# Row standard deviation of an 8192 x 8192 matrix: a column split between VectorE and ScalarE, shrinking last pieces, contiguous loads, and results transposed on TensorE

## The chip, the core and the metric

The kernel runs on one core of a Trainium2 chip. Times are device microseconds (us), and a kernel's time is the median of several executions. The span is the time from the first to the last instruction in the profiled execution; here the median time is about 1.8 us more than the span. All runs that are compared are fast ones, with a granted clock of 1.0.

The program runs on several chips of the same kind, and the kernel before took 641.6, 642.6, 644.6 and 644.8 us in the four jobs of this study. So each variant is set beside the kernel before of its own job.

## The reference

```python
x = np.random.randn(8192, 8192).astype(np.float32)
def reference(x):
    return np.std(x, axis=1)
```

The input has 268.4 MB, the output 32 KB. Everything hangs on how fast x comes in (the page of the kernel before shows the DMA engines at 9 tenths or more in 38 of 40 slices), and on how little is left to do when its last byte has come.

## The kernel before

Partition p holds rows p*64 to p*64+63. One load brings row p*64+i of all 128 partitions, 4 MiB in 128 runs of 32 KiB that lie 2 MiB apart in memory. VectorE sums each row, ScalarE sums its squares in two halves. The last row comes as two halves.

```python
xrows = x.rearrange("(p i) m -> i p m", p=P, i=I)      # P = 128, I = 64, C = 8192, CS = 4096
out_pi = out.rearrange("(p i) -> p i", p=P)
rows = [(i, [0, C]) for i in range(I - 1)] + [(I - 1, [0, CS, C])]     # (shortened)
xpool = ctx.enter_context(tc.tile_pool(name="xtiles", bufs=5))
def do_row(i, cuts):
    # ...
    xt = xpool.tile([P, C], FP32, name="xt")
    for ci in range(len(cuts) - 1):
        c0, c1 = cuts[ci], cuts[ci + 1]
        nc.sync.dma_start(out=xt[:, c0:c1], in_=xrows[i][:, c0:c1])
        nc.vector.reduce_sum(out=asum[:, i - base, ci:ci + 1], in_=xt[:, c0:c1], axis=mybir.AxisListType.X)
        # ... for each piece of up to 4096 columns:
            nc.scalar.activation(out=dummy[:, 0:step], in_=xt[:, s0:s0 + step],
                                 func=Square, accum_out=asq[:, i - base, ci + si:ci + si + 1])
# ... variance of rows 0 to 61 on GpSimd while the last rows load; rows 62 and 63 on VectorE
nc.sync.dma_start(out=out_pi[:, 0:NB], in_=stdA)       # NB = 62: 128 runs of 248 bytes
# ...
nc.scalar.dma_start(out=out_pi[:, NB:I], in_=stdB)     # the last output: 128 writes of 8 bytes, 256 bytes apart
```

## Time and profile before

| | before |
|---|---|
| median time | 642.6 us (641.1 to 643.3, 4 runs) |
| span | 641.0 us |
| spacing of row tiles in the steady part | 9.72 us for 4 MiB |
| VectorE work for a tile | 8.69 us |
| ScalarE work for a tile | 2 x (3.59 + 0.19) us |
| last output, issue to end of span | 2.4 us |

From the page: the busy tenths of the 16 DMA engines and the rate in 40 equal slices of the span.

```profile
DMA  8999999999999999999999999999999999999992
GB/s 339 413 419 405 429 433 433 431 432 429 431 433 433 431 429 431 433 433 431 429 431 425 429 428 436 433 430 431 427 438 431 431 431 427 438 431 431 429 422 88
```

The load is busy from end to end: from the fifth slice to the last but one, the slices read 422 to 438 GB/s, and stretches of 80 to 160 us in the steady part 431 to 433. Only the first four slices (64 us, 339 to 419 GB/s) and the last one are slower. So I counted on no gain in the steady part. That was an estimate: no trace shows how far the rate could rise.

The two costly groups of the page: line, engine, operation, operands and count; busy time and mean of one in ns; idle time of the engine just before them and what ended it.

```profile
L58 DVE TENSOR_REDUCE sumA<-xt 128x1 f32<-128x8192 f32 x62 | 538.5, 8686 | 79.8 <-DMA xt<-in_x_dram 79.8
L67 ACT ACTIVATE dummy<-xt 128x4096 f32<-128x4096 f32 x128 | 459.2, 3587 | 156.1 <-DMA xt<-in_x_dram 154.0
```

Both engines wait for the load at each tile. They are off the critical path until the last tiles. (The page's chain still gives VectorE's reduces 16.3%, because a load is issued when a reduce has freed its buffer. But a load then takes 39.8 us from issue to landing, the time of four tiles, and the DMA engines' share is 0.98 to 1.01 in all stretches from 16 to 625 us: they have work queued throughout.)

VectorE's timeline at the start: start, duration, instruction, and in brackets the idle time before it.

```profile
14.14 8.69 DVE L58 TENSOR_REDUCE sumA<-xt 128x1 f32<-128x8192 f32 x1 [13.22 <-DMA xt<-in_x_dram]
25.27 8.69 DVE L58 TENSOR_REDUCE sumA<-xt 128x1 f32<-128x8192 f32 x1 [2.44 <-DMA xt<-in_x_dram]
34.98 8.69 DVE L58 TENSOR_REDUCE sumA<-xt 128x1 f32<-128x8192 f32 x1 [1.03 <-DMA xt<-in_x_dram]
45.23 8.69 DVE L58 TENSOR_REDUCE sumA<-xt 128x1 f32<-128x8192 f32 x1 [1.56 <-DMA xt<-in_x_dram]
55.51 8.69 DVE L58 TENSOR_REDUCE sumA<-xt 128x1 f32<-128x8192 f32 x1 [1.59 <-DMA xt<-in_x_dram]
66.17 8.69 DVE L58 TENSOR_REDUCE sumA<-xt 128x1 f32<-128x8192 f32 x1 [1.97 <-DMA xt<-in_x_dram]
75.89 8.69 DVE L58 TENSOR_REDUCE sumA<-xt 128x1 f32<-128x8192 f32 x1 [1.04 <-DMA xt<-in_x_dram]
```

A start here marks a tile's landing. The distances are 11.1, 9.7, 10.3, 10.3, 10.7 and 9.7 us: the load starts slowly and then runs evenly.

The end, from the timeline (the last three reduces merged, and the last output) and from the page's list of DMA issues (size, us from issue to landing):

```profile
620.38 17.34 DVE L58 TENSOR_REDUCE sumB<-xt 128x1 f32<-128x8192 f32 x3 [1.10 <-DMA xt<-in_x_dram]
638.58 0.37 ACTq L105 DMA_DIRECT2D out_dram<-stdB  x1
...
out_dram<-stdB ACTq DMA_DIRECT2D x1, 1.0 KB, 1.4
```

VectorE works 17.34 us without a pause from the landing of row 62, and the last output follows.

### The profile page before, as it was taken

The page shows a single profiled execution, that of the slowest core. Times are in us where ns is not written, and L with a number is a line of the kernel's source. Part 1 is how long each engine was busy: PE and PEld are TensorE (multiplying, and loading weights), DVE is VectorE, ACT ScalarE, POOL GpSimd, SP SyncE. Part 2 cuts the span into 40 slices and gives each one's busy share as a digit, 9 for nine tenths or more (in the row PEclk, how much of TensorE's full clock was granted, in tenths as well). Part 3 has the DMA queues.
Part 4 walks back from the last instruction along what each step waited for, and adds up shares of the span by engine and source line. Part 5 has one row for each costly group of instructions (what it writes and reads, how often), then busy time and mean ns, then how long its engine had stood idle before and what let it go on. Part 6 is the DMA issues. An engine that isn't in the chain of part 4 may idle for free.

```text
span 641.0 us, 576 instructions
## 1 busy us (share of the span) xinstructions
DVE 556.5 (87%) x72; ACT 477.9 (75%) x260; POOL 1.4 (0%) x8
## 2 busy tenths in 40 slices
DVE  1889889889889898898898898898898988988988
ACT  1767778778778778777787787787787787777886
POOL 0000000000000000000000000000000000000000
DMA  8999999999999999999999999999999999999992
GB/s 339 413 419 405 429 433 433 431 432 429 431 433 433 431 429 431 433 433 431 429 431 425 429 428 436 433 430 431 427 438 431 431 431 427 438 431 431 429 422 88
DMA packets 9653, 268.51 MB, mean 419 GB/s; under 512 B 1328, under 2 KB 1328, under 8 KB 1328
## 3 DMA queue, kind: packets, MB, share of 16 engines
q1 hardware_dynamic: 9504, 268.47, 97.9%
q14 instruction: 5, 0.04, 0.0%
q10 hardware_dynamic: 144, 0.00, 0.0%
HBM read 268.44 MB, written 0.03 MB: 419 GB/s over the span
## 4 chain that ended last, share of the span: by engine, by line
DMA 80%; DVE 19%; issue 1%; SPq 0%; ACT 0%; DVEq 0%
DMA xt<-in_x_dram 80%; DVE sumA L58 16%; DVE sumB L58 2%; SPq L57 0%; ACT stdB L103 0%; DVE vB L96 0%; DVE m L91 0%; DVE tsumB L89 0%; DVE tsqB L87 0%; DVEq L58 0%
## 5 line engine op out<-in xcount | busy, mean ns | idle before, releaser
L58 DVE TENSOR_REDUCE sumA<-xt 128x1 f32<-128x8192 f32 x62 | 538.5, 8686 | 79.8 <-DMA xt<-in_x_dram 79.8
L67 ACT ACTIVATE dummy<-xt 128x4096 f32<-128x4096 f32 x128 | 459.2, 3587 | 156.1 <-DMA xt<-in_x_dram 154.0
L67 ACT ACTIVATION_READ_ACCUMULATOR dummy<-xt 128x1 f32 x128 | 24.0, 187 | 0.0
L58 DVE TENSOR_REDUCE sumB<-xt 128x1 f32<-128x4096 f32 (+1 forms) x3 | 17.3, 5835 | 1.1 <-DMA xt<-in_x_dram 1.1
L103 ACT ACTIVATE stdB<-vB 128x2 f32<-128x2 f32 x1 | 0.2, 204 | 2.8 <-DVE vB L96 2.8
L67 ACT ACT_TABLE_LOAD x1 | 1.3, 1283 | 0.7 <-PEq L120 0.7
L80 POOL TENSOR_TENSOR tsqA<-sqA 128x62 f32<-128x62 f32 x1 | 0.3, 296 | 617.7 <-ACT dummy L67 617.7
L99 ACT ACT_TABLE_LOAD x1 | 1.3, 1283 | 0.0
L99 ACT ACTIVATE stdA<-vA 128x62 f32<-128x62 f32 x1 | 0.3, 257 | 1.0 <-POOL vA L84 1.0
L47 DVE MEMSET sumB<- 128x8 f32 x1 | 0.1, 65 | 0.8 <-PEq L120 0.8
L84 POOL TENSOR_TENSOR vA<-tsqA,t 128x62 f32<-128x62 f32 x1 | 0.3, 317 | 0.1
L82 POOL TENSOR_TENSOR t<-sumA 128x62 f32<-128x62 f32 x1 | 0.3, 295 | 0.9 <-DVE sumA L58 0.9
L83 POOL TENSOR_TENSOR t<-t,invn_t 128x62 f32<-128x62 f32 x1 | 0.3, 291 | 0.1
L96 DVE TENSOR_TENSOR vB<-tsqB,m 128x2 f32<-128x2 f32 x1 | 0.2, 161 | 0.0
L91 DVE SCALAR_TENSOR_TENSOR m<-tsumB 128x2 f32<-128x2 f32 x1 | 0.2, 160 | 0.0
L89 DVE TENSOR_REDUCE tsumB<-sumB 128x2 f32<-128x8 f32 x1 | 0.2, 161 | 0.0
L87 DVE TENSOR_REDUCE tsqB<-sqB 128x2 f32<-128x8 f32 x1 | 0.1, 149 | 0.0
L120 POOL MEMSET const-bfloat16-1.0<- 128x1 bf16 x1 | 0.1, 103 | 0.0
L120 POOL MEMSET const-uint8-127<- 128x1 uint8 x1 | 0.1, 103 | 0.0
L120 POOL MEMSET const-float32-0.0<- 128x1 f32 x1 | 0.1, 99 | 0.2 <-issue 0.2
L120 POOL MEMSET const-float32-1.0<- 128x1 f32 x1 | 0.1, 99 | 0.0
L48 DVE MEMSET sqB<- 128x8 f32 x1 | 0.1, 65 | 0.0
(1 smaller groups left out, 0.1 us busy)
## 6 DMA issues: line engine op xcount, KB each, us to landing
xt<-in_x_dram SPq DMA_DIRECT2D x63, 4096.0 KB, 39.8
xt<-in_x_dram SPq DMA_DIRECT2D x2, 2048.0 KB, 37.6
out_dram<-stdA SPq DMA_DIRECT2D x1, 31.0 KB, 9.8
out_dram<-stdB ACTq DMA_DIRECT2D x1, 1.0 KB, 1.4
```

The lines of the kernel that those rows point to most:

```text
L58: nc.vector.reduce_sum(out=asum[:, i - base, ci:ci + 1], in_=xt[:, c0:c1], axis=mybir.AxisListType.X,)
L67: nc.scalar.activation(out=dummy[:, 0:step], in_=xt[:, s0:s0 + step], func=mybir.ActivationFunctionType.Square, accum_out=asq[:, i - base, ...
L80: nc.gpsimd.tensor_add(tsqA, sqA[:, :, 0], sqA[:, :, 1])
L82: nc.gpsimd.tensor_mul(t0, sumA[:, :, 0], sumA[:, :, 0])
L83: nc.gpsimd.tensor_mul(t0, t0, invn_t.to_broadcast((P, NB)))
L84: nc.gpsimd.tensor_sub(vA, tsqA, t0)
L89: nc.vector.reduce_sum(out=tsumB, in_=sumB, axis=mybir.AxisListType.X)
L91: nc.vector.scalar_tensor_tensor(out=m2, in0=tsumB, scalar=inv_n, in1=tsumB, op0=mybir.AluOpType.mult, op1=mybir.AluOpType.mult,)
L96: nc.vector.tensor_sub(vB, tsqB, m2)
L99: nc.scalar.activation(out=stdA, in_=vA, func=mybir.ActivationFunctionType.Sqrt, scale=inv_n)
L103: nc.scalar.activation(out=stdB, in_=vB, func=mybir.ActivationFunctionType.Sqrt, scale=inv_n)
L120: nc = _bacc.Bacc("TRN2", target_bir_lowering=False, num_devices=1)
```

## The change

Three things change together. First, rows go to partitions as i*128+p, so one load reads 4 MiB in one piece, and results must be transposed (on TensorE) to be written as rows. Second, the columns of each row are split: VectorE takes 5120 as ten bn_stats of 512 (each leaves six numbers per partition) and one bn_aggr (which merges them into mean and variance), ScalarE 3072 (Square and Copy, each with an accumulator). Third, row 62 comes in halves and row 63 in pieces of 2048, 2048, 2048, 1024, 512, 256 and 256 columns, so that little work is left after the last landing. The intent is a faster start, a lighter VectorE and a short tail.

```diff
-    xrows = x.rearrange("(p i) m -> i p m", p=P, i=I)
-    out_pi = out.rearrange("(p i) -> p i", p=P)
+    xr = x.rearrange("(i p) m -> p i m", p=P, i=I)
+    out_ip = out.rearrange("(i p) -> i p", p=P)
+    ACT_ROW = 3072
+    pieces = [(i, 0, C, ACT_ROW) for i in range(I - 2)]
+    pieces += [(I - 2, 0, C // 2, ACT_ROW // 2), (I - 2, C // 2, C // 2, ACT_ROW // 2)]
+    for n, a in ((2048, 512), (2048, 512), (2048, 512), (1024, 0), (512, 0), (256, 0), (256, 0)):
+        pieces.append((LAST, c0, n, a))
+        c0 += n
-    xpool = ctx.enter_context(tc.tile_pool(name="xtiles", bufs=5))
+    bulk = ctx.enter_context(tc.tile_pool(name="bulk", bufs=4))
+    ends = ctx.enter_context(tc.tile_pool(name="ends", bufs=1))
 ... (per piece)
-            nc.vector.reduce_sum(...)
-                nc.scalar.activation(..., func=Square, accum_out=...)     # two of 4096
+        for d0 in range(a, n, F):                                        # F = 512
+            nc.vector.bn_stats(out=bn[:, k * SD:(k + 1) * SD], in_=xt[:, d0:d1])
+        if a:
+            nc.scalar.activation(out=dump[:, :a], in_=xt[:, :a], func=ACTF.Square, accum_out=q_act[:, r, j:j + 1])
+            nc.scalar.activation(out=dump[:, :a], in_=xt[:, :a], func=ACTF.Copy, accum_out=s_act[:, r, j:j + 1])
+        if c0 + n == C and r < LAST:
+            nc.vector.bn_aggr(out=agg[:, r, :], in_=bn)
+        if c0 + n == C and r == LAST - 1:
+            ... (11 small GpSimd operations give the variance of rows 0 to 62)
+            nc.scalar.activation(out=std, in_=t4, func=ACTF.Sqrt, scale=1.0 / N)
+            nc.tensor.transpose(std_ps, std, ident)
+            nc.scalar.copy(out=std_t, in_=std_ps)
+            nc.sync.dma_start(out=out_ip[0:B, :], in_=std_t)             # rows 0 to 62
 ... (ScalarE's part of row 63 joins VectorE's on GpSimd)
+    nc.vector.bn_aggr(out=agg[:, LAST, :], in_=last_bn)
+    nc.scalar.activation(out=stdl, in_=agg[:, LAST, 1:2], func=ACTF.Sqrt)
+    nc.scalar.dma_start(out=out_ip[LAST, :].rearrange("(p o) -> p o", o=1), in_=stdl)
```

Row 63's results are not transposed. They leave from 128 partitions, 4 bytes from each, to 128 addresses in 512 bytes.

More of the change, by code (lines that the diff above doesn't have):

```diff
@@ L9 @@
 FP32 = mybir.dt.float32
+ACTF = mybir.ActivationFunctionType
+ALU = mybir.AluOpType
 @with_exitstack
@@ L23 @@
     N = float(C)
-    inv_n = 1.0 / N
-    CS = C // 2
-    xrows = x.rearrange("(p i) m -> i p m", p=P, i=I)
-    out_pi = out.rearrange("(p i) -> p i", p=P)
-    NB = I - 2
-    rows = []
-    for i in range(I - 1):
-        rows.append((i, [0, C]))
-    rows.append((I - 1, [0, CS, C]))
-    xpool = ctx.enter_context(tc.tile_pool(name="xtiles", bufs=5))
+    F = nc.vector.BN_STATS_FMAX
+    SD = nc.vector.BN_STATS_DIM
+    LAST = I - 1
+    xr = x.rearrange("(i p) m -> p i m", p=P, i=I)
+    out_ip = out.rearrange("(i p) -> i p", p=P)
@@ L37 @@
+    ACT_ROW = 3072
+    pieces = [(i, 0, C, ACT_ROW) for i in range(I - 2)]
+    pieces += [(I - 2, 0, C // 2, ACT_ROW // 2), (I - 2, C // 2, C // 2, ACT_ROW // 2)]
+    c0 = 0
+    for n, a in ((2048, 512), (2048, 512), (2048, 512), (1024, 0), (512, 0), (256, 0), (256, 0)):
+        pieces.append((LAST, c0, n, a))
+        c0 += n
+    N_D = float(C - ACT_ROW)
+    bulk = ctx.enter_context(tc.tile_pool(name="bulk", bufs=4))
+    ends = ctx.enter_context(tc.tile_pool(name="ends", bufs=1))
     stats = ctx.enter_context(tc.tile_pool(name="stats", bufs=1))
+    bnp = ctx.enter_context(tc.tile_pool(name="bnp", bufs=3))
@@ L38 @@
     psum = ctx.enter_context(tc.tile_pool(name="psumdump", bufs=1, space=bass.MemoryType.PSUM))
-    dummy = psum.tile([P, CS], FP32)
-    NT = I - NB
-    sumA = stats.tile([P, NB, 4], FP32)
-    sqA = stats.tile([P, NB, 4], FP32)
-    sumB = stats.tile([P, NT, 4], FP32)
-    sqB = stats.tile([P, NT, 4], FP32)
-    nc.vector.memset(sumB, 0.0)
-    nc.vector.memset(sqB, 0.0)
-    invn_t = stats.tile([P, 1], FP32)
-    nc.vector.memset(invn_t, inv_n)
-    def do_row(i, cuts):
-        asum, asq, base = (sumA, sqA, 0) if i < NB else (sumB, sqB, NB)
-        xt = xpool.tile([P, C], FP32, name="xt")
-        for ci in range(len(cuts) - 1):
-            c0, c1 = cuts[ci], cuts[ci + 1]
-            nc.sync.dma_start(out=xt[:, c0:c1], in_=xrows[i][:, c0:c1])
-            nc.vector.reduce_sum(
-                out=asum[:, i - base, ci:ci + 1],
-                in_=xt[:, c0:c1],
-                axis=mybir.AxisListType.X,
-            )
-            nsub = (c1 - c0 + CS - 1) // CS
-            step = (c1 - c0) // nsub
-            for si in range(nsub):
-                s0 = c0 + si * step
-                nc.scalar.activation(
-                    out=dummy[:, 0:step],
-                    in_=xt[:, s0:s0 + step],
-                    func=mybir.ActivationFunctionType.Square,
-                    accum_out=asq[:, i - base, ci + si:ci + si + 1],
-                )
@@ L74 @@
-    vA = stats.tile([P, NB], FP32)
-    for (i, cuts) in rows:
-        do_row(i, cuts)
-        if i == NB - 1:
-            tsqA = stats.tile([P, NB], FP32)
-            nc.gpsimd.tensor_add(tsqA, sqA[:, :, 0], sqA[:, :, 1])
-            t0 = stats.tile([P, NB], FP32)
-            nc.gpsimd.tensor_mul(t0, sumA[:, :, 0], sumA[:, :, 0])
-            nc.gpsimd.tensor_mul(t0, t0, invn_t.to_broadcast((P, NB)))
-            nc.gpsimd.tensor_sub(vA, tsqA, t0)
-    tsqB = stats.tile([P, NT], FP32)
-    nc.vector.reduce_sum(out=tsqB, in_=sqB, axis=mybir.AxisListType.X)
@@ L88 @@
-    tsumB = stats.tile([P, NT], FP32)
-    nc.vector.reduce_sum(out=tsumB, in_=sumB, axis=mybir.AxisListType.X)
-    m2 = stats.tile([P, NT], FP32)
-    nc.vector.scalar_tensor_tensor(
-        out=m2, in0=tsumB, scalar=inv_n, in1=tsumB,
-        op0=mybir.AluOpType.mult, op1=mybir.AluOpType.mult,
-    )
-    vB = stats.tile([P, NT], FP32)
-    nc.vector.tensor_sub(vB, tsqB, m2)
-    stdA = stats.tile([P, NB], FP32)
-    nc.scalar.activation(out=stdA, in_=vA,
-                         func=mybir.ActivationFunctionType.Sqrt, scale=inv_n)
@@ L101 @@
-    nc.sync.dma_start(out=out_pi[:, 0:NB], in_=stdA)
-    stdB = stats.tile([P, NT], FP32)
-    nc.scalar.activation(out=stdB, in_=vB,
-                         func=mybir.ActivationFunctionType.Sqrt, scale=inv_n)
-    nc.scalar.dma_start(out=out_pi[:, NB:I], in_=stdB)
+    dump = psum.tile([P, ACT_ROW], FP32)
+    agg = stats.tile([P, I, 2], FP32)
+    s_act = stats.tile([P, I, 3], FP32)
+    q_act = stats.tile([P, I, 3], FP32)
+    nc.gpsimd.memset(s_act, 0.0)
+    nc.gpsimd.memset(q_act, 0.0)
@@ new lines @@
+    ident = stats.tile([P, P], FP32)
+    nc.gpsimd.memset(ident, 1.0)
+    nc.gpsimd.affine_select(out=ident, in_=ident, compare_op=ALU.is_equal, fill=0.0,
+                            base=0, pattern=[[-1, P]], channel_multiplier=1)
+    warm = stats.tile([P, 1], FP32)
+    nc.vector.memset(warm, 1.0)
+    nc.scalar.activation(out=warm, in_=warm, func=ACTF.Sqrt)
+    n_last = sum(-(-(n - a) // F) for r, _, n, a in pieces if r == LAST)
+    a_last = float(sum(a for r, _, n, a in pieces if r == LAST))
@@ new lines, with load, g @@
+    last_bn = stats.tile([P, 3 + n_last * SD], FP32)
+    def load(pi):
+        r, c0, n, _ = pieces[pi]
+        if n == C:
+            xt = bulk.tile([P, C], FP32, name="xt")
+        else:
+            xt = ends.tile([P, n], FP32, name=f"xe{pi}")
+        nc.sync.dma_start(out=xt, in_=xr[:, r, c0:c0 + n])
+        return xt
+    tiles = {}
+    bn, k, j = None, 0, 0
+    for pi, (r, c0, n, a) in enumerate(pieces):
+        if n == C:
+            tiles[pi] = load(pi)
+        elif pi not in tiles:
+            for ahead in range(pi, len(pieces)):
+                tiles[ahead] = load(ahead)
+        xt = tiles.pop(pi)
+        if c0 == 0:
+            k, j = 0, 0
+            if r < LAST:
+                bn = bnp.tile([P, (C - ACT_ROW) // F * SD], FP32, name="bn")
+            else:
+                bn = last_bn[:, 3:]
+        for d0 in range(a, n, F):
+            d1 = min(n, d0 + F)
+            nc.vector.bn_stats(out=bn[:, k * SD:(k + 1) * SD], in_=xt[:, d0:d1])
+            k += 1
+        if a:
+            nc.scalar.activation(out=dump[:, :a], in_=xt[:, :a], func=ACTF.Square,
+                                 accum_out=q_act[:, r, j:j + 1])
+            nc.scalar.activation(out=dump[:, :a], in_=xt[:, :a], func=ACTF.Copy,
+                                 accum_out=s_act[:, r, j:j + 1])
+            j += 1
+        if c0 + n == C and r < LAST:
+            nc.vector.bn_aggr(out=agg[:, r, :], in_=bn)
+        if c0 + n == C and r == LAST - 1:
+            B = LAST
+            def g(nm):
+                return stats.tile([P, B], FP32, name=nm)
+            dm, dv = agg[:, 0:B, 0], agg[:, 0:B, 1]
+            ss, qq, t1, t2, t3, t4 = (g(f"g{z}") for z in range(6))
+            nd = stats.tile([P, 1], FP32)
+            nc.gpsimd.memset(nd, N_D)
+            ndb = nd.to_broadcast((P, B))
+            ninv = stats.tile([P, 1], FP32)
+            nc.gpsimd.memset(ninv, 1.0 / N)
+            ninvb = ninv.to_broadcast((P, B))
+            nc.gpsimd.tensor_add(ss, s_act[:, 0:B, 0], s_act[:, 0:B, 1])
+            nc.gpsimd.tensor_add(qq, q_act[:, 0:B, 0], q_act[:, 0:B, 1])
+            nc.gpsimd.tensor_mul(t1, dm, dm)
+            nc.gpsimd.tensor_add(t1, t1, dv)
+            nc.gpsimd.tensor_mul(t1, t1, ndb)
+            nc.gpsimd.tensor_add(t1, t1, qq)
+            nc.gpsimd.tensor_mul(t2, dm, ndb)
+            nc.gpsimd.tensor_add(t2, t2, ss)
+            nc.gpsimd.tensor_mul(t3, t2, t2)
+            nc.gpsimd.tensor_mul(t3, t3, ninvb)
+            nc.gpsimd.tensor_sub(t4, t1, t3)
+            std = stats.tile([P, B], FP32)
+            nc.scalar.activation(out=std, in_=t4, func=ACTF.Sqrt, scale=1.0 / N)
+            std_ps = psum.tile([B, P], FP32)
+            nc.tensor.transpose(std_ps, std, ident)
+            std_t = stats.tile([B, P], FP32)
+            nc.scalar.copy(out=std_t, in_=std_ps)
+            nc.sync.dma_start(out=out_ip[0:B, :], in_=std_t)
+        if r == LAST and pi + 1 < len(pieces) and pieces[pi + 1][3] == 0 and a:
+            sl = stats.tile([P, 2], FP32)
+            an = stats.tile([P, 1], FP32)
+            nc.gpsimd.memset(an, 1.0 / a_last)
+            nc.gpsimd.memset(last_bn[:, 0:1], a_last)
+            nc.gpsimd.tensor_add(sl[:, 0:1], s_act[:, r, 0:1], s_act[:, r, 1:2])
+            nc.gpsimd.tensor_add(sl[:, 0:1], sl[:, 0:1], s_act[:, r, 2:3])
+            nc.gpsimd.tensor_add(sl[:, 1:2], q_act[:, r, 0:1], q_act[:, r, 1:2])
+            nc.gpsimd.tensor_add(sl[:, 1:2], sl[:, 1:2], q_act[:, r, 2:3])
+            nc.gpsimd.tensor_mul(last_bn[:, 1:2], sl[:, 0:1], an)
+            m2 = stats.tile([P, 1], FP32)
+            nc.gpsimd.tensor_mul(m2, last_bn[:, 1:2], sl[:, 0:1])
+            nc.gpsimd.tensor_sub(last_bn[:, 2:3], sl[:, 1:2], m2)
@@ L109 @@
+    nc.vector.bn_aggr(out=agg[:, LAST, :], in_=last_bn)
+    stdl = stats.tile([P, 1], FP32)
+    nc.scalar.activation(out=stdl, in_=agg[:, LAST, 1:2], func=ACTF.Sqrt)
+    nc.scalar.dma_start(out=out_ip[LAST, :].rearrange("(p o) -> p o", o=1), in_=stdl)
 _INS = ['x']
```

## The prediction

> **What bounds it now.** Loading x. The page's slices show the DMA engines at 9 tenths or more in 38 of 40; the table of stretches gives 432 GB/s from 160 to 320 us. In the timeline a row tile (4 MiB) arrives every 9.72 us. VectorE needs 8.69 us for it and ScalarE 2 x (3.59 + 0.19) = 7.6 us, so both wait for the DMA on each tile (idle before the groups: 79.8 and 156.1 us, ended by the DMA). Three pieces make up the 641.0 us span:
> - start: the first reduce begins at 14.1 us and the next come 11.1, 9.7, 10.3, 10.3, 10.7 us apart before the spacing settles at 9.72. The stretches show 340, 412, 420, 406, 428 GB/s up to 80 us. Against 9.72 that loses about 3.5 us, plus about 2 us before the first tile;
> - steady stream: 64 x 9.72 = 622 us;
> - tail: by the bytes in the stretches, data stop at about 628.4 us; I estimate landing at 630 (row 62's reduce started 1.6 us after its bytes by the same count). The other 11 us are VectorE's backlog (8.7 + 4.4 + 4.4 us, ending 637.7), tiny operations, Sqrt, and 2.4 us of output DMA.
>
> **What the change does.** Per row VectorE gets 5120 columns as ten bn_stats of 512. From the reduces (4409 ns for 4096, 8686 for 8192, so 1.044 ns a column plus about 0.13 us) I estimate 0.60 to 0.67 us each, 6.0 to 6.9 us with bn_aggr. ScalarE does 3072 columns twice: 2 x (2.74 + 0.19) = 5.9 us. Both were off the path already: no gain in the steady part. Four buffers still leave two transfers queued.
>
> Layout: a transfer now reads one contiguous 4 MiB instead of 128 rows 2 MiB apart. [...] this load runs at 432 GB/s at that pitch. [...] The layout may recover part of the 3.5 us start loss, whose cause the trace does not show; I count 1.5 us.
>
> Tail: the last row arrives in pieces down to 256 columns, so VectorE ends within about 1 us of landing. But ScalarE works in order: the Sqrt and PSUM copy for rows 0 to 62 stand before row 63's second and third pieces. Row 62 lands 9.7 us before the end; bn_stats 3.4, nine GpSimd operations at 0.37 = 3.4, Sqrt, transpose and copy about 1.5: ScalarE resumes 1.4 us before the last landing, needs 4 x 0.8 us, then GpSimd about 1.5 us, bn_aggr, Sqrt, output 2.5 us: about 6.7 us after landing instead of 11. Gain 4.3 us, less 0.5 us for small pieces.
>
> **Sum.** 642.8 - 4.3 + 0.5 - 1.5 = about 637.5 us; range 632.5 to 640.5. Faster by over 2% 0.05, within 2% 0.93, slower by over 2% 0.02.
>
> **What the profile would show.** Steady spacing still 9.7 us; VectorE about 6.5 us per tile, ScalarE 5.9; first tiles closer together if the layout matters; the chain of waits ending through ScalarE, GpSimd, bn_aggr, Sqrt and the output, 5 to 8 us after the last landing.
>
> **What would make it wrong.** bn_stats at half my rate would make VectorE the limit (over 11 us a tile). [...]

## The result, and the profile after

The changed kernel takes 643.6 us (643.3 to 643.9, 4 runs) against 642.6. The ratio is 1.0021, 95% interval 1.0006 to 1.0036. A ratio is the mean time of one kernel's fast runs over that of the other's of the same rounds, so it is not quite the ratio of the medians. The change gained nothing. The time is above the predicted range of 632.5 to 640.5.

The slices of the DMA engines and the rate:

```profile
DMA  9999999999999999999999999999999999999990
GB/s 372 445 425 423 435 443 429 423 431 439 435 425 427 433 441 431 425 427 437 441 425 427 431 438 433 429 425 433 439 433 427 423 439 439 427 427 431 430 383 11
```

The start is faster (372 and 445 for 339 and 413), and the rate in the steady part is the same (432 GB/s from 80 to 560 us, for 431 to 433). The groups:

```profile
L92 DVE BATCH_NORM_STATS2 bn<-xt 128x6 f32<-128x512 f32 x620 | 373.9, 678 | 213.4 <-DMA xt<-in_x_dram 213.4
L95 ACT ACTIVATE dump<-xt 128x3072 f32<-128x3072 f32 x62 | 169.6, 2735 | 257.7 <-DMA xt<-in_x_dram 257.7
```

VectorE's own work shrank to 6.03 us for ten bn_stats and 0.43 us for bn_aggr per tile, and it waits more (213.4 us before the bn_stats, for 79.8 before the reduces). That was off the path: between the steps described below, tiles still come 9.7 us apart. VectorE's timeline at the start and around one later tile:

```profile
13.07 6.03 DVE L92 BATCH_NORM_STATS2 bn<-xt 128x6 f32<-128x512 f32 x10 [12.13 <-DMA xt<-in_x_dram]
...
51.91 6.03 DVE L92 BATCH_NORM_STATS2 bn<-xt 128x6 f32<-128x512 f32 x10 [3.22 <-DMA xt<-in_x_dram]
...
62.31 6.03 DVE L92 BATCH_NORM_STATS2 bn<-xt 128x6 f32<-128x512 f32 x10 [3.91 <-DMA xt<-in_x_dram]
...
159.47 6.03 DVE L92 BATCH_NORM_STATS2 bn<-xt 128x6 f32<-128x512 f32 x10 [3.22 <-DMA xt<-in_x_dram]
...
170.15 6.03 DVE L92 BATCH_NORM_STATS2 bn<-xt 128x6 f32<-128x512 f32 x10 [4.19 <-DMA xt<-in_x_dram]
```

The fifth tile lands 3.6 us earlier than before (51.91 for 55.51). But where the wait is usually 3.22 us, it is once 3.91 and then, about every 114 us, 4.19: the steps come before the tiles that start at 62.3, 170.2, 287.7, 395.6 and 513.2 us. They cost 0.7 + 4 x 0.97 = 4.6 us. By row 61 the lead is nearly gone: its work starts at 610.32, against 610.60 before.

What comes at these moments? The page lists the trace's DMA queue 14 as "instruction", with packets, MB and share of time. First the changed kernel's lines of 51 to 56 us, then of 163 to 166 us:

```profile
q14 instruction: 1, 0.01, 0.4%
...
q14 instruction: 1, 0.01, 0.7%
```

Each of the two stretches holds one 8 KB instruction packet. The trace's packet records, in the page's clock, put such packets at 52.3, 163.8, 281.4, 389.3, 506.9 and 618.8 us. The first five last 0.32 to 0.33 us, and the next 32 KiB packet of x behind each takes 1.875 us instead of 1.21 (the sixth falls among the small packets of the end): together the 0.97 us of a step (0.32 + 0.66). Up to 507 us they are on average 113.6 us apart; VectorE issues 11 instructions per 9.72 us, so I estimate about 128 of them for a packet, or 64 bytes each (8192 / 128). The page counts ten such packets in all. The other four stand at 124.2, 375.2, 378.7 and 619.9 us, and no step follows the first three of them, although the next packet of x takes 1.59 to 1.63 us there too. They may be other engines' instructions, on DMA engines that were ahead; the records do not name the engine, so this is not shown.

A step would not matter if the load could make it up. It does not: no spacing after a step is under 9.69 us, and the five add up to 4.6 us. I read this as if each DMA engine had a fixed share of every tile, and a tile had landed when the slowest has finished; no run shows the shares. The stretches of 1 us at the end show how unequally the engines finish. The columns are the stretch, its length, busy us of each engine with the number of instructions (VectorE, ScalarE, GpSimd; for the changed kernel TensorE and its weight loads stand in front), clock, share of the DMA engines, GB/s; first the kernel before:

```profile
627.00:628.00 1.00, 1.00 (x1) 1.00 (x2) 0.00 (x0) 1.00 0.86 352
628.00:629.00 1.00, 1.00 (x2) 0.97 (x2) 0.00 (x0) 1.00 0.41 161
629.00:630.00 1.00, 1.00 (x2) 1.00 (x1) 0.00 (x0) 1.00 0.13 42
630.00:631.00 1.00, 1.00 (x1) 1.00 (x1) 0.00 (x0) 1.00 0.00 0
```

and the changed kernel:

```profile
624.00:625.00 1.00, 0.00 (x0) 0.00 (x0) 1.00 (x3) 0.97 (x4) 1.00 (x5) 1.00 0.83 288
625.00:626.00 1.00, 0.00 (x0) 0.00 (x0) 0.46 (x1) 0.11 (x1) 0.92 (x5) 1.00 0.14 55
...
627.00:628.00 1.00, 0.04 (x1) 0.00 (x0) 0.92 (x2) 0.89 (x4) 0.00 (x0) 1.00 0.06 25
...
629.00:630.00 1.00, 0.00 (x0) 0.00 (x0) 1.00 (x3) 0.97 (x3) 0.19 (x1) 1.00 0.06 23
630.00:631.00 1.00, 0.00 (x0) 0.00 (x0) 1.00 (x3) 0.22 (x2) 0.48 (x3) 1.00 0.05 18
```

A share of 0.06 is one engine in 16 (the stretch at 628 us, left out, also carries the first output). Fourteen engines are done by about 625.3 us, one more at 627.0, and one alone goes on until 630.8 us. Before, they all end between 627.2 and 629.9 us. (Single engines are not named in the records; these ends come from sorting the packets into 16 nearly gapless chains.)

The tail, from the timeline, and the landing of the last output:

```profile
628.51 4.31 DVE L92 BATCH_NORM_STATS2 last_bn<-xe 128x6 f32<-128x512 f32 x8 [0.59 <-DMA xe<-in_x_dram]
...
632.93 0.55 DVE L147 BATCH_NORM_AGGREGATE agg<-last_bn 128x2 f32<-128x87 f32 x1
633.51 0.20 ACT L149 ACTIVATE stdl<-agg 128x1 f32<-128x1 f32 x1 [3.29 <-DVE agg L147]
633.74 0.37 ACTq L150 DMA_DIRECT2D out_dram<-stdl  x1
...
out_dram<-stdl ACTq DMA_DIRECT2D x1, 0.5 KB, 7.3
```

The last output is issued 4.84 us earlier than before (633.74 for 638.58). It then takes 7.3 us to land instead of 1.4, and the span ends 8.20 us after the issue instead of 2.45. So the balance is -4.84 + 5.75 = +0.91 us, which is the difference of the spans.

The theories, from these readings:

- A: 128 small writes that lie side by side in memory finish slowly. Rivals: 4-byte writes are slow anywhere, or the output waits behind the other one.
- B: the layout takes away the slow start. Rival: contiguous loads also bring the steps.
- C: the steps are VectorE's instructions, fetched over a DMA engine that loads x. Rival: they come from bn_stats, four buffers or small pieces.

### The profile page after: what moved, and what is told of

It is laid out like the page before. It is cut to its first block, busy times and chain, and to the rows that moved or that the text cites. A ratio compares the mean times of both kernels' runs of the same rounds, so it can differ in the third digit from the quotient of the medians.

```text
span 641.9 us, 1261 instructions
## 1 busy us (share of the span) xinstructions
PE 0.5 (0%) x1; PEld 0.2 (0%) x1; DVE 415.3 (65%) x709; ACT 366.9 (57%) x273; POOL 5.6 (1%) x30
## 4 chain that ended last, share of the span: by engine, by line
DMA 84%; DVE 14%; SPq 0%; issue 0%; ACT 0%; DVEq 0%
DMA xt<-in_x_dram 77%; DVE bn L92 13%; DMA xe<-in_x_dram 7%; DVE last_bn L92 1%; SPq L72 0%; DVE agg L147 0%; ACT stdl L149 0%; DVEq L147 0%
## 5 line engine op out<-in xcount | busy, mean ns | idle before, releaser
L92 DVE BATCH_NORM_STATS2 bn<-xt 128x6 f32<-128x512 f32 x620 | 373.9, 678 | 213.4 <-DMA xt<-in_x_dram 213.4
L95 ACT ACTIVATE dump<-xt 128x3072 f32<-128x3072 f32 x62 | 169.6, 2735 | 257.7 <-DMA xt<-in_x_dram 257.7
L97 ACT ACTIVATE dump<-xt 128x3072 f32<-128x3072 f32 x62 | 169.6, 2735 | 1.9
L101 DVE BATCH_NORM_AGGREGATE agg<-bn 128x2 f32<-128x60 f32 x63 | 26.8, 426 | 2.2
L95 ACT ACTIVATION_READ_ACCUMULATOR dump<-xt 128x1 f32 x62 | 11.6, 186 | 0.0
L97 ACT ACTIVATION_READ_ACCUMULATOR dump<-xt 128x1 f32 x62 | 11.5, 186 | 0.0
L92 DVE BATCH_NORM_STATS2 last_bn<-xe 128x6 f32<-128x512 f32 (+1 forms) x14 | 8.1, 642 | 1.2 <-DMA xe<-in_x_dram 1.2
L92 DVE BATCH_NORM_STATS2 bn<-xe 128x6 f32<-128x512 f32 x10 | 6.1, 674 | 0.4 <-DMA xe<-in_x_dram 0.4
L95 ACT ACTIVATE dump<-xe 128x512 f32<-128x512 f32 (+1 forms) x5 | 4.7, 941 | 1.2 <-DMA xe<-in_x_dram 1.1
L97 ACT ACTIVATE dump<-xe 128x512 f32<-128x512 f32 (+1 forms) x5 | 4.7, 943 | 0.2
L95 ACT ACTIVATION_READ_ACCUMULATOR dump<-xe 128x1 f32 x5 | 0.9, 187 | 0.0
L97 ACT ACTIVATION_READ_ACCUMULATOR dump<-xe 128x1 f32 x5 | 0.9, 186 | 0.0
```

The source lines that it names most:

```text
L92: nc.vector.bn_stats(out=bn[:, k * SD:(k + 1) * SD], in_=xt[:, d0:d1])
L95: nc.scalar.activation(out=dump[:, :a], in_=xt[:, :a], func=ACTF.Square, accum_out=q_act[:, r, j:j + 1])
L97: nc.scalar.activation(out=dump[:, :a], in_=xt[:, :a], func=ACTF.Copy, accum_out=s_act[:, r, j:j + 1])
L101: nc.vector.bn_aggr(out=agg[:, r, :], in_=bn)
```

## The experiments

### Theory A: the last output

**a_last_pe** transposes row 63's results too, so that they leave as 512 bytes from one partition.

```diff
-    nc.scalar.dma_start(out=out_ip[LAST, :].rearrange("(p o) -> p o", o=1), in_=stdl)
+    stdl_ps = psum.tile([1, P], FP32)
+    nc.tensor.transpose(stdl_ps, stdl, ident)
+    stdl_t = stats.tile([1, P], FP32)
+    nc.scalar.copy(out=stdl_t, in_=stdl_ps)
+    nc.scalar.dma_start(out=out_ip[LAST:LAST + 1, :], in_=stdl_t)
```

> The changed kernel with one edit: the last 128 results are also transposed on TensorE, so they leave as one run of 512 bytes instead of 128 writes of 4 bytes that lie side by side. Theory A (adjacent 4-byte writes of one 512-byte stretch finish slowly): the output takes 1.4 to 2.5 us from issue to landing instead of 7.3; about 1.1 us of transpose, copy and hand-overs is added; the time falls by 4 to 5 us, to about 639. Rival (any small output after this load stream, or one behind the other output, is slow): the landing stays at about 7 us and the time rises by about 1 us.

Measured: correct, 638.23 us (638.03 to 638.27), against 643.58 of the changed kernel in its own job and 644.8 of the kernel before in this one (ratio 0.9882, interval 0.9857 to 0.9907). That is 5.4 us less (different jobs), a little more than expected. The four steps of 0.97 us stay. The page gives no landing for this output; from its issue at 634.34 us to the end of the span (636.3) it is 2.0 us.

**a_last_scatter** keeps the 128 writes of 4 bytes but puts them 256 bytes apart, with a wrong result.

```diff
-    nc.scalar.dma_start(out=out_ip[LAST, :].rearrange("(p o) -> p o", o=1), in_=stdl)
+    nc.scalar.dma_start(out=out.rearrange("(p i) -> p i", p=P)[:, LAST:LAST + 1], in_=stdl)
```

> The changed kernel with the same 128 writes of 4 bytes, but to addresses 256 bytes apart (wrong result on purpose). Theory A [...]: landing falls from 7.3 to about 1.4 us, time falls by about 6 us to 637.7. Rival (4-byte writes are slow by themselves): landing stays near 7 us, time unchanged at about 643.6.

Measured: 637.86 us (637.70 to 638.07). The output's line, from the page's list of DMA issues:

```profile
out_dram<-stdl ACTq DMA_DIRECT2D x1, 0.5 KB, 1.4
```

The same number of 4-byte writes behind the same other output lands in 1.4 us. Both rivals fall: with the addresses adjacent the landing took 7.3 us, and 256 bytes apart 1.4.

**b_contig** is the opposite: the kernel before, with its 128 writes of 8 bytes put side by side (wrong result).

```diff
-    nc.scalar.dma_start(out=out_pi[:, NB:I], in_=stdB)
+    nc.scalar.dma_start(out=out[R - 2 * P:R].rearrange("(p o) -> p o", o=2), in_=stdB)
```

> The kernel before with only the address of its last output changed: its 128 writes of 8 bytes go to one contiguous 1 KB instead of 256 bytes apart (wrong result on purpose). Theory A (adjacent small writes finish slowly): landing rises from 1.4 us to 4 to 8 us and the time by the same 3 to 6 us. Rival (what matters is the changed kernel's other output in front, or the 4-byte size): landing stays at 1.4 us, time unchanged.

Measured: 643.74 us (643.48 to 644.05) against 641.64 (ratio 1.0033, interval 1.0018 to 1.0048). The landing:

```profile
out_dram<-stdB ACTq DMA_DIRECT2D x1, 1.0 KB, 2.9
```

The direction is right and the size was missed: 2.9 us, not 4 to 8 (the time rose by 2.1 us, not 3 to 6). Three more single runs (one profile each) asked how far apart the writes must be. Their outputs are wrong, which doesn't matter for the times. In each, the changed kernel's 4-byte writes go to every 8, 16 or 64 bytes:

```diff
+    nc.scalar.dma_start(out=out[0:P * i].rearrange("(p i) -> p i", i=i)[:, 0:1], in_=stdl)   # i = 2, 4, 16
```

> The changed kernel, its last 128 writes of 4 bytes placed 8 bytes apart (64 of them in each 512 bytes; wrong result on purpose). If only the density of writes in a stretch of memory counts, the landing is about the 2.9 us of b_contig (8-byte writes, 8 bytes apart). If the 4-byte size counts as well, it is nearer to 7.3 us.

> The same, 16 bytes apart (32 writes in each 512 bytes; wrong on purpose). If density counts: between 1.5 and 2.5 us to landing.

> The same, 64 bytes apart (8 writes in each 512 bytes; wrong on purpose). If density counts: 1.4 to 1.7 us, as at 256 bytes apart. [...]

The output's lines in a_step8 and in a_step16 (that of a_step64 reads like a_step16's):

```profile
out_dram<-stdl ACTq DMA_DIRECT2D x1, 0.5 KB, 2.9
...
out_dram<-stdl ACTq DMA_DIRECT2D x1, 0.5 KB, 1.4
```

| 128 writes, one every | size of one | landing |
|---|---|---|
| 4 bytes (changed kernel) | 4 B | 7.3 us |
| 8 bytes (a_step8) | 4 B | 2.9 us |
| 8 bytes (b_contig) | 8 B | 2.9 us |
| 16 bytes (a_step16) | 4 B | 1.4 us |
| 64 bytes (a_step64) | 4 B | 1.4 us |
| 256 bytes (before; a_last_scatter) | 8 B; 4 B | 1.4 us |

Their times were 639.5, 637.9 and 637.7 us. Each landing is read from one profile. In them the distance decides and not the size: 4 and 8 bytes at the same distance take the same (2.9 us at 8 bytes, 1.4 at 256). At 16 bytes' distance the writes landed slightly sooner than expected (1.4 us for 1.5 to 2.5). Why adjacent writes land later was not shown. The runs show only the times: in the changed kernel the packets themselves were through 1.1 us after the issue, and the rest of the 7.3 us passed before the landing was reported.

### Theory B: the layout

**b_layout** is the kernel before with one line changed. Results come out in permuted order on purpose; the check passed it all the same, since the standard deviations of all rows are close to 1.

```diff
-    xrows = x.rearrange("(p i) m -> i p m", p=P, i=I)
+    xrows = x.rearrange("(i p) m -> i p m", p=P, i=I)
```

> The kernel before with only the rows that it loads changed (row i*128+p on partition p, contiguous 4 MiB; the result is permuted on purpose). Theory B (the layout removes the slow packets of the first 65 us; what the changed kernel loses later is not the layout's): first reduce at about 13.1 us instead of 14.1, every spacing 9.7 us from the second tile on, no repeated 1 us steps; time falls by 4 to 4.5 us to about 638.3. Rival (contiguous reads themselves bring the repeated 0.97 us steps of the changed kernel): five steps of 1 us at intervals of about 110 us, time about 642 to 643.

Measured: 638.80 us (638.74 to 638.98) against 644.8 of the same job (ratio 0.9892, interval 0.9867 to 0.9917), and 3.8 us under the 642.6 of the first job. The second tile starts at 22.86 us and the spacing stays at 9.7 us up to the 38th tile; around it 0.1, 0.6 and 0.2 us are lost. There are no regular steps. The layout alone does what was hoped of it, and the rival falls.

**a_layout** is the changed kernel with the old rows:

```diff
-    xr = x.rearrange("(i p) m -> p i m", p=P, i=I)
+    xr = x.rearrange("(p i) m -> p i m", p=P, i=I)
```

> The changed kernel with only the rows that it loads put back (row p*64+i on partition p, 2 MiB apart; outputs as changed, so the result is permuted on purpose). Theory B (the layout is worth the start loss and nothing else): slow packets of up to 2 us again in the first 65 us, the steps of 0.97 us at intervals of about 110 us stay, the slow output stays; time 3.5 to 6 us above the changed kernel, 647 to 650. Rival (the steps come with the contiguous layout): no steps, time about 643 or less.

Measured: 650.86 us (649.96 to 652.68) against 641.64 (ratio 1.0153, interval 1.0130 to 1.0177). The slow start returns (second to sixth tile at distances of 11.3, 9.7, 10.2, 9.6, 10.2 us), and late steps of 0.9 to 1.0 us stay (three, from 289.7 us on, for five in the changed kernel; why the first two are missing was not shown). The time is slightly more than expected, for a reason nobody had named: VectorE's timeline at the end.

```profile
626.76 1.88 DVE L92 BATCH_NORM_STATS2 last_bn<-xe 128x6 f32<-128x512 f32 x3 [0.89 <-DMA xe<-in_x_dram]
631.71 1.88 DVE L92 BATCH_NORM_STATS2 last_bn<-xe 128x6 f32<-128x512 f32 x3 [3.07 <-DMA xe<-in_x_dram]
634.71 4.31 DVE L92 BATCH_NORM_STATS2 last_bn<-xe 128x6 f32<-128x512 f32 x8 [1.12 <-DMA xe<-in_x_dram]
```

The pieces of 2048 columns, 1 MiB each, come 4.95 and 3.0 us apart. In the changed kernel, where their rows are 32 KiB apart instead of 2 MiB, they come 2.47 us apart (626.04 and 628.51). With runs of 8 KiB the pitch of 2 MiB cost time at the end too (4.95 and 3.0 us for 2.47), so here the shrinking pieces need the new layout.

### Theory C: the instruction fetches

**b_layout_dve** adds ten tiny memsets per row on VectorE to b_layout, so that VectorE has about as many instructions (712) as in the changed kernel (709).

```diff
+    pad = stats.tile([P, 1], FP32)
     for (i, cuts) in rows:
         do_row(i, cuts)
+        for _ in range(10):
+            nc.vector.memset(pad, 0.0)
```

> The run b_layout plus 640 tiny memsets on VectorE (ten per row, each about 0.03 us apart; the scheduler packs them into the first 25 rows). Theory C (VectorE's instructions are fetched from memory 128 at a time over one of the DMA engines that load x; each fetch sets that engine back by about 1 us for good): about five more 8 KB instruction packets than in b_layout, five steps of about 1 us in the tile spacing within the first 25 rows, time 4.5 to 5 us above b_layout. Rival (the steps belong to bn_stats, to four buffers or to the small last pieces): no steps, time within 0.7 us of b_layout.

Measured: 654.70 us, and it decides nothing. VectorE's timeline:

```profile
107.31 8.68 DVE L58 TENSOR_REDUCE sumA<-xt 128x1 f32<-128x8192 f32 x1
...
119.06 8.68 DVE L58 TENSOR_REDUCE sumA<-xt 128x1 f32<-128x8192 f32 x1
```

There is no idle time in brackets: with 25 or 26 memsets between two reduces, which cost about 0.12 us each instead of the 0.03 that I had read off three at the start, VectorE needs 11.7 us per tile and had become the limit.

**b_layout_pool** therefore puts the same 640 memsets on GpSimd, which has nothing to do with the load. The edit is the same with `nc.gpsimd.memset`.

> The run b_layout plus 640 tiny memsets on GpSimd, an engine that touches nothing of the load; nothing orders them, so they run in the first 70 us or so. (The same on VectorE had made VectorE the limit and so could not decide.) Theory C (instruction fetches in blocks of 128 share a DMA engine with the load and set it back for good): about five more 8 KB instruction packets, all in the first 70 us, up to five steps of about 1 us in the tile spacing there, and a time 3 to 5 us above b_layout's 638.8. Rival (the steps of the changed kernel come from bn_stats, four buffers or small pieces): no steps, time within 0.7 us of 638.8.

Measured: 640.62 us (640.35 to 640.71), 1.8 us above b_layout (different jobs). (Beside the kernel before of its own job, which ran faster at 641.64, its ratio is 0.9983.) It has ten instruction packets of 8 KB for b_layout's five. VectorE's timeline:

```profile
22.90 8.69 DVE L58 TENSOR_REDUCE sumA<-xt 128x1 f32<-128x8192 f32 x1 [1.03 <-DMA xt<-in_x_dram]
33.26 8.69 DVE L58 TENSOR_REDUCE sumA<-xt 128x1 f32<-128x8192 f32 x1 [1.68 <-DMA xt<-in_x_dram]
42.97 8.69 DVE L58 TENSOR_REDUCE sumA<-xt 128x1 f32<-128x8192 f32 x1 [1.03 <-DMA xt<-in_x_dram]
53.34 8.69 DVE L58 TENSOR_REDUCE sumA<-xt 128x1 f32<-128x8192 f32 x1 [1.68 <-DMA xt<-in_x_dram]
63.06 8.69 DVE L58 TENSOR_REDUCE sumA<-xt 128x1 f32<-128x8192 f32 x1 [1.03 <-DMA xt<-in_x_dram]
73.43 8.69 DVE L58 TENSOR_REDUCE sumA<-xt 128x1 f32<-128x8192 f32 x1 [1.68 <-DMA xt<-in_x_dram]
```

Every second tile comes 0.65 us late, four times up to 93.5 us, while GpSimd runs its memsets (0.7 to 101 us). The records put the five extra packets 20 us apart (the first, at 11.0 us, falls before the first tile has landed and shows no step). The 640 memsets took 100.2 us, so 20 us is 128 of them; the memsets themselves ran evenly, 102 or 103 in each 16 us, and I would expect a slowdown by them to be even too, and not one step per 128. After that the spacing is 9.71 us to the end. Memsets on an engine that is otherwise nearly idle slowed a load that they don't touch, by four steps of 0.65 us, with no bn_stats, five buffers and no small pieces: the rival falls. The size was missed. A fetch cost 0.65 us here (0.31 of its own, and the next packet of x 1.57 instead of 1.21), not 1. And b_layout already had a DMA engine that finished late: its slowest ended 1.5 us after the bulk, and in this run the slowest ended 3 us after it. The difference of 1.5 us is nearer to the 1.8 us of the times than the four steps' sum of 2.6. So my estimate is that the largest delay of any one engine counts, and not the sum; no run isolates this.

### All findings together

**best** takes the changed kernel, computes rows 0 to 60 with one reduce on VectorE and one Square over 8192 columns on ScalarE, keeps the split for rows 61 to 63 and their pieces, and transposes the last output. VectorE falls from 709 to 99 instructions and ScalarE from 273 to 152. To make room, row 62's halves share a bulk buffer.

```diff
+    wide = stats.tile([P, C], mybir.dt.bfloat16)
+    nc.gpsimd.memset(agg, 0.0)
+    BODY = I - 3
+        elif r == LAST - 1:
+            if c0 == 0:
+                half.append(bulk.tile([P, C], FP32, name="xt"))
+            xt = half[0][:, c0:c0 + n]
+        if r < BODY:
+            nc.vector.reduce_sum(out=s_act[:, r, 0:1], in_=xt, axis=mybir.AxisListType.X)
+            nc.scalar.activation(out=wide, in_=xt, func=ACTF.Square, accum_out=q_act[:, r, 0:1])
+            continue
 (and the last output as in a_last_pe)
```

> All findings together: contiguous layout; rows 0 to 60 by one tensor_reduce on VectorE and one Square over 8192 columns on ScalarE, so few instructions are fetched; rows 61 to 63 and the shrinking pieces as in the changed kernel; both outputs transposed on TensorE. If theories A, B and C hold: first tile at 13.1 us, spacing 9.72 us with at most one step, all 16 DMA engines done within about 1 us of each other at about 625 us, time 632.5 to 635. If C is wrong and the steps come from elsewhere, the steps stay and the time is about 638, as in a_last_pe.

Measured: correct, 633.46 us (633.36 to 633.69) against 641.64 (ratio 0.9873, interval 0.9858 to 0.9888). This beats both kernels. Its last stretches:

```profile
624.00:625.00 1.00, 0.00 (x0) 0.00 (x0) 0.93 (x2) 0.97 (x3) 0.19 (x1) 1.00 0.87 291
625.00:626.00 1.00, 0.00 (x0) 0.00 (x0) 1.00 (x3) 0.94 (x5) 0.19 (x1) 1.00 0.17 58
626.00:627.00 1.00, 0.00 (x0) 0.00 (x0) 1.00 (x2) 0.70 (x2) 0.34 (x2) 1.00 0.03 10
627.00:628.00 1.00, 0.00 (x0) 0.00 (x0) 1.00 (x4) 0.00 (x0) 0.60 (x4) 1.00 0.00 0
```

All DMA engines are done by 626.3 us; the one that straggled to 630.8 us is gone, although VectorE is busier in this kernel (551 us) than in the changed one (415 us). Over the whole run two spacings are long, by 0.2 and 0.8 us. Compared with a_last_pe, which keeps the many instructions, it is 4.8 us faster (different jobs).

## Why the prediction was wrong

The forecast "within 2%" was right, and the time missed: 643.6 us for a range that ended at 640.5. Point by point:

- *Steady spacing of 9.7 us, no gain from lighter engines.* Right: 9.72 us, and ten bn_stats took 6.03 us (predicted 6.0 to 6.9 with bn_aggr; 6.46). ScalarE took 5.84 (predicted 5.9).
- *"Output 2.5 us."* This is the step that failed. Counted from the issue to the end of the span it was 8.20 us. I took the time of the old output, 128 writes of 8 bytes that lie 256 bytes apart, for 128 writes of 4 bytes that lie side by side. These 5.7 us are nearly the whole miss (643.6 - 637.5 = 6.1). a_last_pe and a_last_scatter give them back.
- *"I count 1.5 us" for the start.* Mis-sized. The fifth tile landed 3.6 us earlier, and without the first step the sixth would have been 4.5 us earlier. b_layout shows the layout to be the cause. Why the old layout is slow only for its first 65 us is open.
- *No cost in the 709 VectorE instructions.* A missing term. Five steps cost 4.6 us up to row 61. They ate the lead of the start, so the wrong sizes of start and steps nearly cancelled.
- *The tail through ScalarE and GpSimd, 6.7 us after landing.* The order of ScalarE's queue was read correctly (row 63's second piece had landed by 626.04 us, and its Square ran at 627.24, behind the Sqrt at 626.26 and the PSUM copy at 627.08), but it did not bind: GpSimd was done with row 63 at 631.36 us, and VectorE, fed by the straggling DMA engine, at 632.82. From a predicted span of about 635.7 us the output would have been issued near 633.2; it was at 633.74. So the sum up to the output was right to half a microsecond, by errors that cancelled.
- *No gain counted from the layout in the steady part.* Right for whole rows: 9.72 us in both kernels, outside the steps. For short pieces a_layout showed a cost of the old layout that I had not counted (1 MiB pieces 4.95 and 3.0 us apart, for 2.47).

Open: why a fetch for VectorE costs 0.97 us and one for GpSimd 0.65 us, and why adjacent writes land later (7.3 us for 1.4).

## What to carry to other kernels

Here a stream kept all DMA engines full, and delays of single engines stayed to the end: one went on to 630.8 us where fourteen were done by 625.3. In a kernel bound like this, look at which engines finish last, and count instructions: best, with 99 VectorE instructions for 709 and 152 ScalarE instructions for 274, was 4.8 us faster than a_last_pe (different jobs). Small results that lie side by side in memory did better as one run (transposed first: 2.0 us from issue to the end of the span, for 8.20) or spread: 128 writes of 4 bytes landed in 1.4 us from 16 bytes' distance on, and adjacent ones in 7.3. When a change does several things and the time stays, look for gains and losses that cancel before calling the parts worthless: here the layout alone was worth 3.8 to 6.0 us.
